# Hybrid GLA and gated-delta layer on one core: length sums in the input stage, delta-rule pairs pipelined by hand, linear attention by units, w_out in halves

## The chip, the core and the metric

The kernel runs on one core of a Trainium2 chip. The time is the device time of one execution in microseconds. The engines are PE (matmuls), PEld (its weight loads), DVE (vector), ACT (activations and copies), POOL (GpSimd) and SP (a queue that issues most DMAs). Each executes its own instructions in order.

## The reference, cut to what matters

One decoder layer for 2048 prompt tokens and 8 samples of 8 tokens (2112 columns). One projection feeds two recurrences: gated linear attention (GLA) and the gated delta rule (GDN). Their outputs are normed, gated and multiplied by `w_out`; a layer norm and a SwiGLU network follow.

```python
h = einsum('btd,de->bte', x, w_in)                    # q,k,v,gates of GLA, conv inputs of GDN, ...
dq = l2_norm(silu(conv(q part))) * DK ** -0.5          # l2_norm: x * rsqrt(sum(x*x) + 1e-6), per head
dk = l2_norm(silu(conv(k part)))
a_mat = eye + strict(beta_i * (k_i . k_j) * exp(gcum_i - gcum_j))
u, w = solve(a_mat, [v * beta, k * beta * exp(gcum)])
delta = u - w @ s
o = (q * exp(gcum)) @ s + (q k^T * gamma) @ delta
s = exp(gcum_last) * s + (k * exp(gcum_last - gcum))^T @ delta
o = rms_norm(o) * silu(gate)
```

## The kernel before, in words

The tokens are cut into 17 units: unit 0 is the 64 sample tokens, units 1 to 16 are 128 prompt tokens each. Eight blocks hold two prompt units each; block 0 also holds unit 0.

The input stage (`phase_in`) goes three times over 704 columns, each in two halves of 352. For each of 12 groups of convolution channels (`f`) and each half, `product` runs 24 matmuls into a PSUM tile `p`. `conv` then copies it to `hb` on ACT, does three multiply-adds into `cv` on DVE, takes Silu on ACT (line 93, `cv<-cv`) and stores it to DRAM. The small columns (decays, beta, gate rank) are a further product of 24 matmuls for each half, into a PSUM tile `g` of which there are two. All other projections follow through `seven` (lines 226 to 228).

The recurrences follow. `phase_gla` and `phase_gdn` are generators that are advanced by turns, one block each. In GDN, `proj` of a block loads q and k, and `unit` makes them of unit length in place, 512 columns at a time:

```python
ptt(sq, x, x, TT.mult)                                        # POOL
nc.tensor.matmul(ps, lhsT=ones, rhs=sq, start=True, stop=True) # PE, line 811
act(rt, ps, AF.Ln, bias=epsl)                                 # ACT
act(rt, rt, AF.Exp, scale=-0.5, bias=lnq[:, g:g + 1])         # ACT
vtt(x, x, rt, TT.mult)                                        # DVE
```

`decays` reads the summed log decays back from DRAM to all partitions (`R`) and takes exponents. `prepare` makes the matrices of a unit (`y`, `yh`, `at`, `kh`, `ke`, `qe`), with k k^T, q k^T and transposes through the one PSUM bank `sc`. `invert` is called for seven levels, for the two units of a block by turns: a matmul group, a copy to `P` on ACT (line 888), two matmul groups, and two predicated copies on DVE (lines 897 and 898). `residual` (its copy `Rs`) and `correct` finish the inverse, and `advance` carries the state through the unit. The tiles `yh`, `yl`, `D` and `DT` have two buffers each, so a block's inversion needs the block ahead of it to be through with them.

The output stage (`phase_out`) loads `w_out` in eight chunks through the two staging buffers `wraw`, scales each on DVE and splits it in a high and a low half (`o0h`, `o0l`, `o1h`, `o1l`), then handles the units in order (`project`). `phase_ffn` is the rest.

The program text sets the order of emission, but a scheduler of the framework reorders the instructions of each engine by its own timing; data and buffers bound it.

Of the kernel before, what the change touches and what calls it, by code (L numbers as in the profile page):

```python
# [20 lines left out]
NS = 64  # L21
# [79 lines left out]
def hybrid_layer(ctx: ExitStack, tc: tile.TileContext, I, O):  # L101
# [41 lines left out]
    if "og" in O:  # L143
# [3 lines left out]
                             for nm, n in (("qk", 4), ("v", 4), ("gt", 8), ("dq", 12)))  # L147
    sm_d = dram.tile([40, NTOK], F32, name="sm")
    grow_d = [dram.tile([4, T], F32, name=f"gr_{b}") for b, (_, T, _) in enumerate(blocks)]
# [9 lines left out]
    c_nb = cols.tile([128, NU, 4], F32, name="c_nb")  # L159
    c_G = cols.tile([64, 4], F32, name="c_G")  # L160
# [5 lines left out]
    def load_quad(pool, tag, src, gain):  # L166

        wh, wl = (pool.tile([128, 8, 512], F32R, name=tag + p, tag=tag + p, bufs=1) for p in "hl")
# [7 lines left out]
        return wh, wl  # L176
# [91 lines left out]
    def phase_in(stack):  # L268
# [52 lines left out]
        def conv(ib, i, f, ps):  # L321
# [23 lines left out]
            nc.scalar.dma_start(out=dq_d[f][:, t0:t0 + FN], in_=cv)  # L345

# [5 lines left out]
        for ib in range(3):  # L352
            if ib:
                ws = load_pair(pw, I["w_p"][0], plain=True)
                xs = load_x(ib)
            for p in range(6):
                if p:
                    ws = load_pair(pw, I["w_p"][p], plain=True)
                for j, c in enumerate("ab"):
                    w = [cols_of(ws[c + d]) for d in "12"]  # L360
                    for i in range(2):
                        ps = psp.tile([128, 512], F32, name="p", tag="p")[:, :FN]
                        product(ps, w, i)
                        conv(ib, i, 2 * p + j, ps)
# [15 lines left out]
            for i in range(2):  # L380
                ps = psg.tile([128, 512], F32, name="g", tag="g")[:64, :FN]
                product(ps, [[(lambda k, d=d, t=t: t[:, 4 * d + k, :]) for t in (wsh, wsl)] for d in range(2)], i)
                sm = p4.tile([64, FN], F32, name="sm", bufs=1)
                nc.scalar.copy(sm, ps)
                t0 = FT * ib + FN * i
                ST.dma_start(out=sm_d[:, t0:t0 + FN], in_=sm[:40])
# [7 lines left out]
        ST.dma_start(out=O["pconv"].rearrange("(f p) c -> p f c", p=128), in_=halo)  # L394


    def phase_gla(stack, more=None, general=False):
# [19 lines left out]
        if not general:  # L417

            gsc = w1.tile([40, 3], F32, name="gsc")
            nc.sync.dma_start(out=gsc[32:40, :], in_=I["gates"])  # L420
            nc.vector.tensor_tensor(gsc[32:40, 1:2], gsc[32:40, 1:2], gsc[32:40, 0:1], op=TT.mult)
            act(gsc[32:40, 2:3], gsc[32:40, 2:3], AF.Exp)
# [18 lines left out]
        if not general:  # L441
            ats = [p1.tile([128, 4, 128], F32, name=f"at{i}", bufs=1) for i in range(2)]
            lows = p1.tile([128, 2, 24], F32, name="lows", bufs=1)

            grs = p1.tile([128, 320], F32, name="grs", bufs=1)
            for t in ats + [lows, grs]:
# [8 lines left out]
        def log_sig(w, rows, T, nm):  # L455

            e = p1.tile([128, 320], F32, name="ls_" + nm, tag="ls", bufs=1)[rows, :T]
            act(e, w, AF.Abs)
            nc.vector.tensor_scalar(w, w, 0.0, None, op0=TT.min)
            act(e, e, AF.Exp, scale=-1.0)  # L460
            act(e, e, AF.Ln, bias=1.0)
            return e

        def proj(b):
# [4 lines left out]
            if not general:  # L469
                wr = p1.tile([40, 320], F32, name="wr", bufs=1)  # L470
                R8 = slice(32, 40)
                nc.sync.dma_start(out=wr[R8, :T], in_=sm_d[32:40, c0:c0 + T])
                nc.vector.tensor_scalar(wr[R8, :T], wr[R8, :T], gsc[R8, 0:1], gsc[R8, 1:2],
                                        op0=TT.mult, op1=TT.add)
                lr = p1.tile([40, 320], F32, name="lr", bufs=1)
                vtt(lr[R8, :T], wr[R8, :T], log_sig(wr[R8, :T], R8, T, "r"), TT.subtract)
                nc.vector.tensor_scalar(lr[R8, :T], lr[R8, :T], gsc[R8, 2:3], None, op0=TT.mult)
                gr = grs
# [828 lines left out]
```

## Time and profile before

| what | us |
|---|---|
| median of three runs (2832.56, 2833.11, 2841.64) | 2833.11 |
| the profiled execution, device time | 2829.82 |
| its span, first to last instruction | 2827.7 |
| PE busy in the span | 2665.6 |
| input stage, to | 633 |
| recurrences, from 633 to | 1113 |
| output stage, from 1113 to | 1384 |
| feed-forward stage, from 1384 to | 2828 |

The stage borders are read from the timeline: the last input product on PE, the first transpose of the output stage, the first product of the feed-forward network. A busy PE holds the modelled length of each matmul, so a PE that is busy in part of a stretch may also be waiting for the clock. PEclk of 1.00 is 2.4 GHz and 0.50 is 1.2 GHz.

### The profile page before, as it was taken

Reading aid. Unit: us, or ns where it says so; the run is one execution under the profiler, and the core shown is the slowest. Engines: PE = TensorE matmul, PEld = TensorE weight load, DVE = VectorE, ACT = ScalarE, POOL = GpSimd, SP = SyncE. Lnnn points to the kernel's source line nnn. Section 1 sums busy time; section 2 is a strip of 40 time slices with the busy share of each in tenths; the row PEclk is TensorE's granted clock in tenths of the full one; section 3 lists DMA queues with packets and bytes.
Section 4 is the critical chain, followed back from the end, with each engine's and each line's share of the span. In section 5 each row is a group of like instructions: output and inputs, shape, how many; then the busy total and the mean of one; then the engine's idle time right before and its main releaser. Section 6 shows DMA issues by size and latency. Waiting matters only on the chain.

```text
span 2827.7 us, 45495 instructions
## 1 busy us (share of the span) xinstructions
PE 2665.6 (94%) x16362; PEld 2435.2 (86%) x16362; DVE 1982.8 (70%) x3160; ACT 1241.3 (44%) x2660; POOL 1176.9 (42%) x1185
## 2 busy tenths in 40 slices
PE   8999999997888887999799999999999999999996
PEld 8999999995767675777799999999999987887885
DVE  7868768655678766686677788777877743555664
ACT  5545445434455553343344453444444432334442
POOL 6534325324344431354555559655665500210111
PEclk9999999996899998999899999999999999999998
DMA  7345344324533223667732346323432243536652
GB/s 258 126 152 186 121 144 157 108 101 126 148 98 99 65 70 102 188 205 240 239 117 101 112 147 203 114 101 124 140 107 103 100 144 131 202 131 244 214 200 85
DMA packets 244232, 406.60 MB, mean 144 GB/s; under 512 B 27900, under 2 KB 202460, under 8 KB 223132
## 3 DMA queue, kind: packets, MB, share of 16 engines
q1 hardware_dynamic: 195900, 364.22, 39.0%
q10 hardware_dynamic: 48096, 39.38, 4.2%
q8 instruction: 131, 2.15, 0.3%
q14 instruction: 105, 0.86, 0.1%
HBM read 305.01 MB, written 98.51 MB: 143 GB/s over the span
## 4 chain that ended last, share of the span: by engine, by line
PE 48%; DMA 2%; DVE 2%; POOL 1%; issue 1%; ACT 0%; SPq 0%; POOLq 0%; ACTq 0%; DVEq 0%
PE p L227 10%; PE p L228 10%; PE p L226 10%; PE p L1203 4%; PE p L1205 4%; PE p L1204 4%; PE g L1203 2%; PE g L1205 2%; PE g L1204 2%; DMA x1T<-x1T 1%; DMA xr<-x1T 1%; POOL xr L131 1%; DVE xl L128 0%; DMA wr<-in_w_dn 0%; DVE wl L128 0%
## 5 line engine op out<-in xcount | busy, mean ns | idle before, releaser
L128 DVE TENSOR_TENSOR wl<-wr,wh 128x512 fp32r<-128x512 f32 x652 | 595.1, 916 | 337.8 <-ACT wh L182 335.4
L226 PE MATMUL p<-xh,wh 128*128 128x352 f32 x2520 | 814.3, 323 | 10.2 <-ACT x1T L1096 5.0
L227 PE MATMUL p<-xl,wh 128*128 128x352 f32 x2520 | 815.1, 323 | 4.1 <-DVE xl L128 4.1
L228 PE MATMUL p<-xh,wl 128*128 128x352 f32 x2520 | 814.4, 323 | 0.3 <-DVE wl L128 0.3
L182 ACT CAST wh<-wr 128x512 fp32r<-128x512 f32 x652 | 401.1, 620 | 582.1 <-PE p L227 274.8
L226 PEld LDWEIGHTS p<-xh,wh 128*128 128x128 f32 x2520 | 474.6, 188 | 11.6 <-ACT x1T L1096 5.4
L227 PEld LDWEIGHTS p<-xl,wh 128*128 128x128 f32 x2520 | 474.8, 188 | 5.9 <-DVE xl L128 5.6
L228 PEld LDWEIGHTS p<-xh,wl 128*128 128x128 f32 x2520 | 474.8, 188 | 0.8 <-DVE wl L128 0.8
L128 DVE TENSOR_TENSOR t<-t,p 128x352 f32<-128x352 f32 x630 | 318.7, 518 | 199.0 <-PE p L228 197.3
L131 POOL TENSOR_TENSOR wt<-wr 128x512 f32<-128x512 f32 x180 | 243.9, 1355 | 242.8 <-DVE wl L128 211.7
L182 ACT CAST wh<-wt 128x512 fp32r<-128x512 f32 x270 | 167.5, 621 | 311.7 <-PE p L227 280.5
L1028 POOL TENSOR_SCALAR mv<-mv 128x1 f32<-128x1 f32 (+1 forms) x34 | 22.8, 674 | 505.6 <-DVE mv L1027 505.6
L128 DVE TENSOR_TENSOR wl<-wt,wh 128x512 fp32r<-128x512 f32 x270 | 202.7, 751 | 19.0 <-ACT wh L182 15.8
L1203 PE MATMUL p<-wh,hh 128*128 128x512 f32 x528 | 208.8, 395 | 0.0
L1204 PE MATMUL p<-wl,hh 128*128 128x512 f32 x528 | 208.7, 395 | 0.0
L131 POOL TENSOR_TENSOR wt<-wr,wt 128x512 f32<-128x512 f32 x90 | 119.4, 1326 | 212.2 <-DVE wl L128 212.0
L1205 PE MATMUL p<-wh,hl 128*128 128x512 f32 x528 | 204.5, 395 | 0.0
L316 PE MATMUL p<-xh,wh 128*128 128x352 f32 x576 | 186.2, 324 | 10.9 <-ACT xh L182 10.9
L317 PE MATMUL p<-xl,wh 128*128 128x352 f32 x576 | 186.3, 323 | 0.0
L318 PE MATMUL p<-xh,wl 128*128 128x352 f32 x576 | 186.2, 323 | 0.0
L131 POOL TENSOR_TENSOR t<-t 128x352 f32<-128x352 f32 x132 | 159.5, 1210 | 59.4 <-ACT t L93 35.3
L332 DVE SCALAR_TENSOR_TENSOR cv<-hb,cw,cv 128x352 f32<-128x352 f32 (+1 forms) x216 | 153.3, 715 | 40.2 <-ACT cv L330 22.6
(280 smaller groups left out, 4816.1 us busy)
## 6 DMA issues: line engine op xcount, KB each, us to landing
wr<-in_w_gu SPq DMA_DIRECT2D x66, 1024.0 KB, 4.9
wr<-in_w_dn SPq DMA_DIRECT2D x55, 1024.0 KB, 4.9
wr<-in_w_p SPq DMA_DIRECT2D x42, 1024.0 KB, 5.1
hid<-t SPq DMA_DIRECT2D x132, 176.0 KB, 1.8
xr<-in_xT SPq DMA_DIRECT2D x96, 176.0 KB, 4.6
dq<-cv ACTq DMA_DIRECT2D x72, 176.0 KB, 2.9
xr<-x1T SPq DMA_DIRECT2D x72, 176.0 KB, 3.6
hr<-hid SPq DMA_DIRECT2D x66, 192.0 KB, 3.4
```

The costliest lines, as they stand in the source:

```text
L128: nc.vector.tensor_tensor(out, a, b, op=op)
L131: nc.gpsimd.tensor_tensor(out, a, b, op=op)
L182: nc.scalar.copy(h[:, :N], raw)
L226: nc.tensor.matmul(ps, lhsT=h[:, ks], rhs=x[k][0], start=k == 0, stop=False)
L227: nc.tensor.matmul(ps, lhsT=h[:, ks], rhs=x[k][1], start=False, stop=False)
L228: nc.tensor.matmul(ps, lhsT=l[:, ks], rhs=x[k][0], start=False, stop=k == 3)
L316: nc.tensor.matmul(ps, lhsT=h(k), rhs=x[k][0], start=n == 0, stop=False)
L317: nc.tensor.matmul(ps, lhsT=h(k), rhs=x[k][1], start=False, stop=False)
L318: nc.tensor.matmul(ps, lhsT=l(k), rhs=x[k][0], start=False, stop=n == 7)
L1203: nc.tensor.matmul(p, lhsT=hh[:, ts], rhs=wd[i][0], start=f == 0, stop=False)
L1204: nc.tensor.matmul(p, lhsT=hh[:, ts], rhs=wd[i][1], start=False, stop=False)
L1205: nc.tensor.matmul(p, lhsT=hl[:, ts], rhs=wd[i][0], start=False, stop=f == NF - 1)
```

## The change

It has four parts.

1. Length sums. `lengths` squares each of the first eight `cv` tiles of a half on ACT and adds the sums of its 128 rows into one row of a PSUM tile `g`, by a matmul with a selector of 8 columns. `store_rows` stores the eight rows to DRAM (`nm`). `rows` takes their logarithm and adds minus half of it to the log decays (in the rows that go to `R`, and in the columns `c_nb`), so that k and q needn't be scaled. What that leaves unscaled in q is put right in the norm of the output stage (`c_r`, `c_rq`). `unit` is gone.
2. GDN pairs. `mix` is replaced by a loop over groups (pairs of units, and the sample unit as the fourth group): between the two `advance` calls of a group four steps of the next group's inversion are emitted, and the group after that is prepared at the end. `yh`, `yl`, `D`, `DT` and `P` have four buffers now. q, k and v are loaded by the unit.
3. GLA advances by units; its sample unit comes after the eighth prompt unit.
4. `w_out` has two pools. The first half is loaded from `phase_gdn`, one chunk after each group; the second in the output stage.

```diff
+        def lengths(f, nps, cv):
+            sq = p4.tile([128, FN], F32, name="sq")
+            nc.scalar.activation(sq, cv, AF.Square)
+            r = (f + 4) % 8
+            nc.tensor.matmul(nps[:8, :FN], lhsT=sel[:, 7 - r:15 - r], rhs=sq, start=f == 0, stop=f == 7)
...
+        def rows(b):
...
+            act(nr[R8, :T], nr[R8, :T], AF.Ln, bias=epsl[R8])
...
+            nc.vector.scalar_tensor_tensor(rr[R4, :T], nr[R4, :T], -0.5, grs[R4, :T], op0=TT.mult, op1=TT.add)
+            for u in us:
+                u0, C = units[u]
+                o = u0 - c0
+                ST.dma_start(out=grow_d[u][:, 0:C], in_=rr[R4, o:o + C])
+                ST.dma_start(out=grow_d[u][:, C:], in_=grs[R4, 7:64:8] if u == 0 else grs[R4, o + C - 1:o + C])
...
+                nc.vector.scalar_tensor_tensor(nb, ct[:C, 64:68], -0.5, ct[:C, 36:40], op0=TT.mult, op1=TT.add)
+                vtt(nb, nb, ct[:C, 0:4], TT.subtract)
...
+                vtt(c_r[:C, u, :], ct[:C, 64:68], ct[:C, 68:72], TT.subtract)
+                act(c_rq[:C, u, :], c_r[:C, u, :], AF.Exp, scale=0.5, bias=lnq[:C])
+                ptt(c_r[:C, u, :], c_rq[:C, u, :], c_rq[:C, u, :], TT.mult)
...
-            def unit(x, N, g):
-                sq = pe.tile([128, 512], F32, name="sq")[:, :N]
-                ptt(sq, x, x, TT.mult)
-                ps = bank("sc")[:, :N]
-                nc.tensor.matmul(ps, lhsT=ones, rhs=sq, start=True, stop=True)
...
+        for n, us in enumerate(groups):
+            if n + 2 < len(groups) and blk[n + 2] > 1:
+                rows(blk[n + 2])
+            steps = inversion(groups[n + 1]) if n + 1 < len(groups) else iter(())
+            for i, u in enumerate(us):
+                for _ in range(4):
+                    next(steps, None)
+                if u == 0:
+                    advance_samples(ws.pop(u))
+                else:
+                    advance(u, ws.pop(u))
+                yield
+            for _ in steps:
+                pass
+            next(more, None)
+            start(n + 2)
...
-            return pa.tile([128, FN], F32, name="xr", bufs=8)
+            return pa.tile([128, FN], F32, name="xr", bufs=7)
```

What that does to the engines' orders shows at three places. First PE at the start of the program, before the change; `p` is a convolution product, `g` the small columns.

```order
L316 MATMUL p<-xh,wh 128x352
L316 MATMUL g<-xh,wsh 64x352
L317 MATMUL p<-xl,wh 128x352
L318 MATMUL p<-xh,wl 128x352
L316 MATMUL p<-xh,wh 128x352
L317 MATMUL g<-xl,wsh 64x352
L317 MATMUL p<-xl,wh 128x352
L318 MATMUL p<-xh,wl 128x352
```

Of the change, the place on PE where the first row of length sums stands, after 43 matmuls of products; `sel` is the selector.

```order
L319 MATMUL p<-xl,wh 128x352
L320 MATMUL p<-xh,wl 128x352
L360 MATMUL g<-sq,sel 8x352
L319 MATMUL p<-xl,wh 128x352
L320 MATMUL p<-xh,wl 128x352
L318 MATMUL p<-xh,wh 128x352 x2
```

The length sums hold both `g` tiles until the eighth channel group is done, so the 24 matmuls of the small columns that stood among the first 60 stand behind the 16th sum now. Each of the 48 sums stands among later products: in the second and third pass 43 to 62 product matmuls behind the last one of its own product.

Next PE in the recurrences of the change: the end of the eighth GLA unit (`g<-v,kz` is its state update), with GDN's state products (`seq`, `po`) and k k^T of the samples (`sc<-k`) around it.

```order
L920 MATMUL seq<-S,ke 128x128 x4
L836 MATMUL sc<-k 64x64 x2
L644 MATMUL g<-v,kz 128x128 x4
L936 MATMUL po<-S,qe 128x128
L528 MATMUL g<-ident,vf 64x128
L890 LDWEIGHTS P_7796
L890 MATMUL inv<-D,P_7796 128x64
```

The recurrences take some 3700 rows of PE's order. The next GLA prompt unit (its gate product `g<-gar,wup`) stands some 1800 rows further on; between them GLA has its sample unit only, and GDN goes on alone. The other eight GLA units stand behind that, the last two behind GDN's last state update. Before, GLA's 16 units stood among the first five GDN blocks, and the last three had none beside them.

Last SP in the recurrences: of the change, the third chunk of `w_out` (`Sh` and `state_gdn` are the samples' state, which uses the same two staging buffers).

```order
L525 DMA vf<-v 128x4x128
L486 DMA gar_8631<-sm 16x256
L174 DMA wraw<-in_w_out 128x2x512
L947 DMA Sh<-in_state_gdn 128x8x128
L754 DMA wr<-sm 8x256
L772 DMA gr_111<-grs 4x8x1
```

Two chunks stand in the input stage, this one near the start of the recurrences, the fourth in their middle, and four (the second half) behind that. Before, the first two of the eight chunks stood among the loads of the last GDN block, and the rest in the output stage:

```order
L798 DMA vf<-dq 128x4x128 x2
L790 DMA cv<-dq 128x4x256
L172 DMA wraw<-in_w_out 128x2x512 x2
L1047 DMA lng<-in_ln 128x1024
L1048 DMA lnb<-in_ln 128x1024
L172 DMA wraw<-in_w_out 128x2x512
```

## Rows read from the trace of the kernel before

**Rows 1.** The page: span, and engines' busy time.

```profile
span 2827.7 us, 45495 instructions
PE 2665.6 (94%) x16362; PEld 2435.2 (86%) x16362; DVE 1982.8 (70%) x3160; ACT 1241.3 (44%) x2660; POOL 1176.9 (42%) x1185
```

**Rows 2.** Busy time of each engine by stage; PEclk is the granted clock.

```profile
core 0: us, PE busy (x) PEld busy (x) DVE busy (x) ACT busy (x) POOL busy (x), PEclk, DMA share, GB/s
0.00:50.00 50.00, 38.83 (x225) 37.28 (x226) 35.09 (x65) 29.84 (x70) 27.07 (x41) 1.00 0.81 286
50.00:633.00 583.00, 583.00 (x3647) 580.04 (x3646) 438.38 (x691) 283.21 (x584) 237.96 (x291) 1.00 0.42 139
633.00:1113.00 480.00, 392.26 (x3618) 331.04 (x3616) 339.11 (x733) 237.20 (x587) 183.57 (x263) 0.88 0.34 97
1113.00:1384.00 271.00, 237.29 (x1100) 185.32 (x1100) 189.87 (x265) 108.85 (x366) 122.54 (x138) 0.93 0.71 218
```

**Rows 3.** The same, stretches of the recurrences.

```profile
633.00:735.00 102.00, 82.80 (x535) 63.23 (x533) 53.52 (x120) 38.45 (x98) 38.92 (x74) 0.72 0.45 126
...
773.00:941.00 168.00, 138.31 (x1332) 119.47 (x1331) 136.64 (x295) 100.89 (x258) 71.84 (x104) 0.95 0.33 94
...
1002.00:1113.00 111.00, 88.27 (x1002) 76.83 (x1000) 72.92 (x162) 48.96 (x112) 29.84 (x35) 0.95 0.23 69
```

**Rows 4.** Timeline of PE in the recurrences: start, length, instruction.

```profile
1014.14 1.02 PE L811 MATMUL sc<-sq,ones 128*128 128x512 f32 x2
1015.00 0.39 PE L937 MATMUL po<-S,qe 128*128 128x128 f32 x2
```

**Rows 5.** Timeline of PE in the input stage.

```profile
233.84 0.32 PE L316 MATMUL p<-xh,wh 128*128 128x352 f32 x1
234.00 0.32 PE L317 MATMUL p<-xl,wh 128*128 128x352 f32 x1
```

**Rows 6.** Timeline of ACT in the input stage, second pass, first and third product.

```profile
227.37 0.45 ACT L327 COPY hb<-p 128x352 f32<-128x352 f32 x1
...
232.56 0.50 ACT L93 ACTIVATE cv<-cv 128x352 f32<-128x352 f32 x1 [0.84 <-DVE cv L332]
...
244.58 0.50 ACT L93 ACTIVATE cv<-cv 128x352 f32<-128x352 f32 x1 [2.18 <-DVE cv L332]
```

**Rows 7.** PE's groups and waits between 8 and 30 us.

```profile
L316 PE MATMUL p<-xh,wh 128*128 128x352 f32 x26 | 8.8, 353 | 10.9 <-ACT xh L182 10.9
...
L316 PE MATMUL g<-xh,wsh 128*64 128x352 f32 x8 | 3.2, 396 | 0.2 <-ACT wsh L306 0.2
```

**Rows 8.** Groups of DVE, POOL and ACT in the recurrences: busy, mean ns | idle before.

```profile
L128 DVE TENSOR_TENSOR cv<-cv,rt 128x512 f32<-128x512 f32 x32 | 25.6, 799 | 13.3 <-ACT rt L93 10.5 <-issue 1.8 <-POOL ckh L131 0.7
...
L473 DVE TENSOR_SCALAR wr<-wr,gsc 8x256 f32<-8x256 f32 x7 | 4.1, 587 | 1.4 <-DMA wr<-sm 1.3
...
L128 DVE TENSOR_TENSOR ckh<-sc,c_nb 64x4 f32<-64x4 f32 x1 | 0.1, 144 | 0.0
...
L131 POOL TENSOR_TENSOR sq<-cv 128x512 f32<-128x512 f32 x32 | 34.5, 1081 | 39.9 <-PE sc L811 23.1 <-PE sc L801 14.4 <-PE inv L884 2.3
...
L131 POOL TENSOR_TENSOR ckh<-R,c_nb 128x4 f32<-128x4 f32 x16 | 3.4, 218 | 21.9 <-DVE kh L128 19.5 <-DMA R<-gr 2.2
...
L93 ACT ACTIVATE rt<-rt,lnq 128x512 f32<-128x512 f32 x32 | 23.3, 728 | 0.4
```

**Rows 9.** Timeline of PE, start of the output stage; in brackets the wait.

```profile
1113.00 0.69 PE L1073 MATMUL pt<-ident,on 64*128 64x64 f32 x4 [4.33 <-DVE on L128]
...
1135.79 0.69 PE L249 MATMUL pw<-o1h,oh 128*64 128x512 f32 x1 [3.87 <-ACT o1h L174]
...
1141.65 0.45 PE L249 MATMUL pw<-o0h,oh 128*128 128x512 f32 x1
```

**Rows 10.** DMA issues in the recurrences (KB each, us to landing), then the chain that ended last.

```profile
R<-gr SPq DMA_DIRECT2D x16, 256.0 KB, 3.2
...
1689.10 3.29 DMA xr<-x1T
```

More of the change, by code (lines that the diff above doesn't have):

```diff
@@ L380, in phase_in @@
             for i in range(2):
[L381 to L386, printed above, removed]
+                ps = psg.tile([128, 512], F32, name="g", tag="g")
+                product(ps[:64, :FN], [[(lambda k, d=d, t=t: t[:, 4 * d + k, :]) for t in (wsh, wsl)] for d in range(2)], i)
+                store_rows(ps, 64, sm_d, ib, i)
             for n, (to, c) in enumerate(dst):
@@ L706, in phase_gla @@
         for b in range(NBLK):
-            mix(b, proj(b))
-            yield
+            r = proj(b)
+            if b == 0:
+                r0 = r
+            yield from mix([u for u in blocks[b][2] if u], r)
+            if b == 3:
+                yield from mix([0], r0)
         S = state["S"]
@@ L828, in prepare @@
[L828 removed]
+            return gbt[:C, :, :C], eR[:, :, :C], ckh, eGl
+        def prepare(u):
             u0, C = units[u]
             smp = u == 0
[L832 to L834 removed]
+            w = {}
+            q, k, vf = (new(n)[:, :, :C] for n in ("q", "k", "vf"))
+            for t, n in ((q, 0), (k, 4), (vf, 8)):
+                nc.sync.dma_start(out=t, in_=dq_d[n:n + 4, :, u0:u0 + C].rearrange("h p t -> p h t"))
+            w["q"], w["k"] = q, k
+            gb, eR, ckh, w["eGl"] = decays(u)
+            w["eR"] = eR
+            pt = pmt("sc")
+            for h in range(4):
+                nc.tensor.transpose(pt[:C, h, :], vf[:, h, :], ident)
+            w["v"] = new("vt")
+            nc.scalar.copy(w["v"][:C], pt[:C])
@@ L1015, in phase_gdn, with inversion @@
-        for b in range(NBLK):
-            mix(b, proj(b))
-            yield
+        ws = {}
+        def inversion(us):
+            C = units[us[0]][1]
+            for lv in range(3 if C == NS else 7):
+                for u in us:
+                    invert(lv, C, ws[u])
+                yield
+            for u in us:
+                residual(C, ws[u])
+            yield
+            for u in us:
+                correct(C, ws[u], "D", "t1", F16)
+            for u in us:
+                correct(C, ws[u], "t1", "Dr", F32)
+            yield
@@ new lines, in phase_gdn, with start @@
+        groups = [[u, u + 1] for u in range(1, NU, 2)]
+        groups.insert(3, [0])
+        blk = [us[0] // 2 for us in groups]
+        def start(n):
+            if n < len(groups):
+                for u in groups[n]:
+                    ws[u] = prepare(u)
+        rows(0)
+        start(0)
+        rows(1)
+        for _ in inversion(groups[0]):
+            pass
+        start(1)
+        for n, us in enumerate(groups):
[5 more added lines that the diff above has]
+                    next(steps, None)
+                if u == 0:
+                    advance_samples(ws.pop(u))
+                else:
+                    advance(u, ws.pop(u))
+                yield
+            for _ in steps:
+                pass
+            next(more, None)
+            start(n + 2)
@@ L1018, in phase_gdn @@
+        for _ in more:
+            pass
         ST.dma_start(out=O["pgdn"].rearrange("h d v -> d h v"), in_=state["S"])
-        yield
     def layer_norm(pool, v, C, g, b, spare=False):
@@ L1238, in hybrid_layer @@
                 pass
-        with ExitStack() as stack:
-            finish(stack)
+        out = ExitStack()
+        wo, more = load_out(out, gain, 0)
+        for _ in more:
+            pass
+        finish(rest, out, wo)
 GT, X1T = 3, 1
```

311 lines of the change are left out of this document (131 added, 180 removed).

## The prediction

> **What bounds the kernel now.** I read the page first [rows 1]: PE is busy for 2665.6 of 2827.7 us, so the question is where it isn't, and whether its busy time is real work. The windows by stage answer that [rows 2]. From 50 to 633 us PE is busy for all of 583 us at a granted clock of 1.00: the input stage is bound by PE, and whatever is added to PE there is paid in full. In the first 50 us PE waits for data (38.8 busy). The recurrences take 480 us, and no engine is full: PE 392 at a mean clock of 0.88, DVE 339 (0.706 of the stretch), ACT 237, POOL 184. That stage is bound by chains that cross engines, and by how well two recurrences fill each other's gaps. Its stretches differ [rows 3]: from 633 to 735, where the samples' chain runs almost alone, DVE is busy for 0.52; from 773 to 941, where GLA and GDN run side by side, 136.64 of 168, or 0.813; from 1002 to the end, where GLA is through and GDN goes alone, 72.92 of 111, or 0.657. The output stage is nearly full of PE work (237 of 271) but for its start and end.
>
> **The change, part by part.** *Length sums added to the input stage.* PE gets 48 matmuls of f32 with 352 columns (8 channel groups, 3 passes, 2 halves). The nearest row is the old sum of squares, f32 with 512 columns in two passes: started at 1014.14, the next instruction at 1015.00 [rows 4], so 0.86 us, or 0.59 for 352 columns; 48 x 0.59 = 28.3 us. A product matmul of 352 columns starts each 0.16 us [rows 5], but it is one pass over operands split in high and low. No row has f32 with eight columns of weights, so the far ends are 48 x 0.16 = 7.7 and 48 x 0.86 = 41; I take 28.3, since passes and columns are the same kind as in rows 4. PE has no gap there to hide it.
>
> *Do these sums wait?* A sum stands 43 to 62 product matmuls behind its own product, so 6.9 to 9.9 us, and up to 1.2 more for sums between. What it needs: the first product of the second pass is read at 227.37, and its Silu ends at 233.06, after 5.7 us. The third product ends 48 x 0.16 = 7.7 us later, at 235.05, and its Silu ends at 245.08, after 10.0 us [rows 6]. The Square adds about 0.5, as long as a Silu. So 6.2 to 10.5 are needed where 6.9 to 11 are given: 3 us of waits in all, between 0 and 8. ACT gets 48 x 0.5 = 24 us in a stage where it is busy for 283 of 583, which hides it; without that cover it would come out as just these waits.
>
> *Small columns later.* While PE waits at the start (10.9 us, for x), 24 matmuls of small columns fill its time (eight in each of three lines) [rows 7]. Their tiles are held by the sums now, so they come in a full stretch: 24 x 0.16 = 3.8 us, less if products move up in their place. Between 0 and 3.8; I take 3. Input stage: 28.3 + 3 + 3 = +34, between +29 and +42 at the price taken.
>
> *Taken out of the recurrences.* POOL loses 32 squares (34.5 us) and two half as wide, ACT 64 activations of some 0.7 us, PE 32 x 0.86 = 27.5 us, DVE 32 multiplies (25.6 us) and two half as wide, 26.4 in all [rows 8]. Added on DVE: one operation of 8 rows for each block at 0.59, so 5 us, and three of four columns for each of 17 units at 0.144, so 7 us. DVE's work goes from 339 to 339 - 26 + 5 + 7 = 325 us. POOL and ACT, at half of the stretch or less, are not what fills it.
>
> *Order of the recurrences.* PE loses 27.5 us of work but wasn't full, so I price the stage by how full DVE gets. By the order, 44 in 100 of DVE's instructions of this stage stand where GLA pauses. The rest, 0.56 x 325 = 182 us, has GLA beside GDN and takes the fill of rows 3, 0.813: 224 us. The paused part, 143 us of work, would at the old fill of GDN alone, 0.657, take 218. Four buffers let a pair's inversion start while the pair ahead is corrected and advanced, and the samples' chain now lies among pairs. I take a fill halfway, 0.735: 195 us. Together 419 in place of 480, so -61. Bounds: 0.813 throughout gives 400 (-80), 0.657 in the pause 442 (-38). What is late next is the end: the last two GLA units stand behind GDN's last state update, with nothing beside them.
>
> *Loads of `w_out`.* In the output stage the first transpose starts at 1113.00, the second unit's products at 1141.65: 28.6 us for a unit where steady ones take some 16 (the stage's 271 us over 17). In it PE waits for the second half's chunks, 3.87 us at most at once [rows 9]. The first half is there in advance now, and two chunks of the second wait in staging. At least that wait goes (-4), at most 28.6 - 16 and the gap of 4.33 ahead (-17); I take -11.
>
> *At no cost.* SP issues 91 DMAs more, and each unit's `R` comes by two stores and a load that lands in 3.2 us [rows 10]; rows are made two groups ahead, which hides it. Without that cover it is about 6 us for each of 8 pairs, and is part of the first rival. The norm of the output stage gets two POOL operations for each unit, 0.22 each [rows 8]; loads run ahead there, and PE is the bound. Uncovered: 17 x 0.44 = 7 us. The feed-forward stage has seven raw buffers instead of eight: its second block now waits 3.29 us for such a load [rows 10], at most as much again at each of two entries.
>
> *Sum.* The profiled execution took 2829.8 us, 2.1 more than its span and 3.3 less than the median of the runs: 2829.8 + 34 - 61 - 11 = 2792, as a median 2795.
>
> *A rule against it.* PE's granted clock is 0.72 from 633 to 735, where its work is sparse, and 0.95 from 773 on [rows 3]; the levels are 1.2 and 2.4 GHz, so it spent more than half of that first stretch at the lower one. The Trainium skill, "TensorE: Matmul & The Clock Gate", Part 1 (the HAM clock gate), says that the throttled rate is the default and that activity releases it. This trace agrees, with 0.72 and 0.95. By that rule the pause of GLA, with less on PE, could go at the lower level for long, and the time would be that of the third rival.
>
> **The rivals.** *First: the hand order brings nothing.* A scheduler already reorders all of it, and the old order too started the next inversion behind the last correction; the pause of GLA makes half of the stage like its old end. Then fill stays at 0.706: 325 / 0.706 = 460, -20. 2829.8 + 34 - 20 - 11 + 3.3 = 2836, no change. Against it: the samples' 102 us at a fill of 0.52 go in among pairs.
>
> *Second, on the other side: the sums stall PE.* PE is in order, so a sum whose Square is late stops all products behind it. If each of 48 comes 1.5 us late, 72 us in place of 3: 2864. For it: needs of up to 10.5 us against places of 6.9 upward [rows 6]. Against it: a stall gives DVE and ACT time to catch up. It decides from 50 us of waits, 1 us for each sum.
>
> *Third: the clock falls in the pause.* If the paused 195 us go at 0.72 in place of 0.95, they take 257: +62, 2857. It decides at a clock of 0.77 there. For it: PE has neither GLA nor the old sums then. Against it: GDN alone, from 1002 on, has 0.95.
>
> *Fourth: more than forecast.* With inversions of two pairs in flight DVE is full to 0.90 throughout: 361 us, -119, so 2737.
>
> **How the numbers follow.** Forecast 0.62, first rival 0.13, second 0.08, third 0.07, fourth 0.10. The forecast's own range takes the terms' bounds: 2829.8 + 29 - 80 - 17 + 3 = 2765 to 2829.8 + 42 - 38 - 4 + 3 = 2833. About 0.3% (8.5 us) is what a measurement can tell from no change. Faster: 0.62 less the 0.02 of its upper end, and 0.10, so 0.70. Same: 0.13 + 0.02, and a small second rival 0.01, so 0.16. Slower: 0.14. The range for 8 in 10 leaves out most of the second and third rivals: 2742 to 2842.
>
> **What would show it.** The input stage should end at 662 to 675, with PE full; 48 sums at 0.59 each, and few waits for the Square. The recurrences should take 400 to 442 us, with GLA absent from the middle, DVE at 0.7 or more there and at 0.8 at both ends, and no sum on POOL. The first output unit should take under 20 us, and the feed-forward stage its 1444 us. I am wrong if sums wait for ACT by over 1 us each, if the middle's clock is under 0.8, or if the stage's DVE fill stays at 0.7.

## The result: slower by 2.6%, and the profile after

The changed kernel takes 2912.11 us (median of 2908.22 to 2917.14), the kernel before 2835.01 on the same chip: a ratio of 1.0262 with a 95% interval of 1.0246 to 1.0278. Forecast were 2795, with 0.14 for slower. Its profiled execution has a span of 2909.4 us; these are its page's first lines, which answer to [rows 1].

```profile
span 2909.4 us, 45610 instructions
PE 2687.0 (92%) x16390; PEld 2447.1 (84%) x16390; DVE 1964.3 (68%) x3185; ACT 1235.3 (42%) x2671; POOL 1134.2 (39%) x1197
```

DVE lost 18 us of work, PE gained 21, and the span grew by 82: most of that is neither. The windows by stage, as in [rows 2] (busy time of each engine with its instructions, PEclk, DMA share, GB/s), show where.

```profile
0.00:50.00 50.00, 31.78 (x166) 29.21 (x167) 33.54 (x57) 26.87 (x63) 22.03 (x40) 0.93 0.80 276
50.00:692.00 642.00, 635.74 (x3819) 594.34 (x3818) 442.76 (x702) 312.48 (x648) 225.60 (x295) 1.00 0.38 127
692.00:1162.00 470.00, 368.77 (x3533) 327.41 (x3531) 326.36 (x763) 209.83 (x547) 153.29 (x237) 0.84 0.39 106
1162.00:1472.00 310.00, 250.91 (x1089) 197.30 (x1090) 175.40 (x252) 98.75 (x353) 123.62 (x167) 0.88 0.58 174
1472.00:2373.00 901.00, 888.13 (x5545) 885.40 (x5544) 700.70 (x990) 398.95 (x727) 541.20 (x410) 0.99 0.37 127
2373.00:2909.00 536.00, 511.67 (x2246) 413.42 (x2244) 285.56 (x423) 188.41 (x336) 68.45 (x52) 0.98 0.49 173
```

To compare kernels, the stages are cut at the same events on PE in each: the last product of the input stage, the first transpose of the output stage (a wait ahead of it counts with the recurrences), the first gate product, the first down product. Us, from the timelines:

| kernel | input | recurrences | output | gate and up | down | median, ratio to before (95%) |
|---|---|---|---|---|---|---|
| before | 635.9 | 477.2 | 261.7 | 904.5 | 548.5 | 2835.01 |
| after | 691.9 | 470.1 | 309.7 | 901.4 | 536.3 | 2912.11, 1.0262 |
| difference | +56.0 | -7.0 | +48.0 | -3.1 | -12.2 | forecast: +34, -61, -11, 0, 0 |

Where PE waits in the whole of the changed kernel (sum, times, longest):

```profile
PE pw L251 <- ACT oh L1109: 50.9, 16, 10.2
PE p L318 <- ACT xh L184: 17.6, 2, 8.9
PE pt L1104 <- DVE on L128: 15.4, 2, 12.6
...
PE g L360 <- ACT sq L358: 6.5, 11, 1.4
```

The second is the wait for x at the start, 10.9 before [rows 7]; the third is the output stage's start, the last the length sums. The first, 16 times in the 17 units of the output stage, is new: one of them lasts 10.2 us, the others 2.7 on average (before, there were two such waits, 4.4 us in all). The timeline of PE there shows it; a period is from one `px` row to the next, 17.37 us.

```profile
1241.81 1.03 PE L1125 MATMUL px<-ident,xt 128*128 128x128 f32 x8
1245.71 1.03 PE L1104 MATMUL pt<-ident,on 128*128 128x128 f32 x8
1249.42 0.80 PE L251 MATMUL pw<-o0h,oh 128*128 128x512 f32 x1 [2.68 <-ACT oh L1109]
...
1259.18 1.03 PE L1125 MATMUL px<-ident,xt 128*128 128x128 f32 x8
...
1263.08 1.03 PE L1104 MATMUL pt<-ident,on 128*128 128x128 f32 x8
```

Before, the same rows of two units, with other rows of PE left out; the period is 12.95 us:

```profile
1164.41 1.03 PE L1094 MATMUL px<-ident,xt 128*128 128x128 f32 x8
1166.68 0.60 PE L1073 MATMUL pt<-ident,on 128*128 128x128 f32 x4
1169.92 0.60 PE L1073 MATMUL pt<-ident,on 128*128 128x128 f32 x4
1177.36 1.03 PE L1094 MATMUL px<-ident,xt 128*128 128x128 f32 x8
```

There the transposes come in two groups of four, each among the products of the unit ahead, and wait for nothing. After the change, all eight transposes `pt` of a unit stand right before that unit's own products `pw`, so the gating on DVE and the split to `oh` on ACT lie open between them. That was to be read from the order of the changed kernel before it ran, and the prediction took no notice of it.

And the length sum, in the input stage. It has two records (x2) and lies between the products of 302.12 and 303.06, which stand 0.94 apart in place of 0.16: 0.78 for a sum, not 0.59. All 37 sums that didn't wait cost the same.

```profile
302.12 0.32 PE L319 MATMUL p<-xl,wh 128*128 128x352 f32 x1
302.37 0.76 PE L360 MATMUL g<-sq,sel 128*8 128x352 f32 x2
303.06 0.43 PE L320 MATMUL p<-xh,wl 128*128 128x352 f32 x1
```

### The profile page after: what moved, and what is told of

It reads as the page before. It is cut to its first block, busy times and chain, and to the rows that moved or that the text cites. A ratio compares the mean times of both kernels' runs of the same rounds, so it can differ in the third digit from the quotient of the medians.

```text
span 2909.4 us, 45610 instructions
## 1 busy us (share of the span) xinstructions
PE 2687.0 (92%) x16390; PEld 2447.1 (84%) x16390; DVE 1964.3 (68%) x3185; ACT 1235.3 (42%) x2671; POOL 1134.2 (39%) x1197
## 5 line engine op out<-in xcount | busy, mean ns | idle before, releaser
L228 PEld LDWEIGHTS p<-xh,wh 128*128 128x128 f32 x2520 | 474.3, 188 | 10.2 <-ACT xh L184 5.3
```

Source lines behind the costliest of these rows:

```text
L228: nc.tensor.matmul(ps, lhsT=h[:, ks], rhs=x[k][0], start=k == 0, stop=False)
```

## The experiments

The table has all eighteen, the columns as above.

| run | input | recurrences | output | gate and up | down | median | ratio (95%) |
|---|---|---|---|---|---|---|---|
| a_on3 | 692.6 | 471.7 | 249.0 | 902.6 | 536.1 | 2851.96 | 1.0058 (1.0040 to 1.0076) |
| a_pipe | 692.2 | 472.0 | 255.7 | 902.6 | 534.4 | 2858.05 | 1.0081 (1.0052 to 1.0110) |
| a_sides | 691.6 | 462.4 | 309.6 | 900.4 | 546.6 | 2912.91 | 1.0285 (1.0244 to 1.0326) |
| b_sides | 639.1 | 503.6 | 258.3 | 915.0 | 534.0 | 2849.96 | 1.0049 (1.0032 to 1.0066) |
| a_sumr | 667.4 | 476.7 | 306.4 | 900.1 | 536.4 | 2891.56 | 1.0217 (1.0191 to 1.0243) |
| a_noord | 691.9 | 473.2 | 307.6 | 900.9 | 535.5 | 2907.55 | 1.0267 (1.0241 to 1.0293) |
| a_noord2 | 693.2 | 482.2 | 306.7 | 900.8 | 534.6 | 2923.88 | 1.0339 (1.0300 to 1.0378) |
| a_glaend | 693.9 | 477.8 | 311.9 | 902.2 | 535.5 | 2919.55 | 1.0310 (1.0284 to 1.0336) |
| a_unit | 638.2 | 478.6 | 304.0 | 900.9 | 537.9 | 2860.76 | 1.0088 (1.0066 to 1.0111) |
| a_early | 692.1 | 459.8 | 249.8 | 902.6 | 536.4 | 2839.49 | 1.0022 (1.0002 to 1.0042) |
| a_best | 658.4 | 470.0 | 251.9 | 902.6 | 535.9 | 2819.08 | 0.9932 (0.9913 to 0.9950) |
| a_best2 | 657.7 | 465.6 | 249.8 | 903.2 | 538.0 | 2812.16 | 0.9912 (0.9893 to 0.9930) |
| a_unit2 | 638.5 | 467.8 | 255.2 | 902.0 | 535.2 | 2804.96 | 0.9908 (0.9889 to 0.9926) |
| a_nogla | 692.8 | 407.3 | 309.9 | 899.8 | 537.0 | 2849.51 | 1.0046 (1.0018 to 1.0074) |
| a_inv3 | 693.7 | 465.9 | 304.0 | 901.6 | 536.9 | 2902.82 | 1.0247 (1.0217 to 1.0276) |
| a_sc2 | 693.6 | 460.9 | 307.4 | 902.5 | 535.2 | 2901.27 | 1.0241 (1.0212 to 1.0271) |
| a_warm | 692.0 | 465.3 | 308.5 | 901.6 | 539.6 | 2912.22 | 1.0281 (1.0262 to 1.0299) |
| a_final | 637.4 | 464.9 | 255.8 | 901.5 | 535.9 | 2798.71 | 0.9872 (0.9851 to 0.9893) |

### The output stage: one buffer, or the order written out

```diff
-                on = pi.tile([128, 512], F32, name="on", bufs=2)
+                on = pi.tile([128, 512], F32, name="on", bufs=3)
```

> The changed kernel with one more buffer for the loaded outputs (on, three in place of two), nothing else. In the order of PE each unit's transposes then stand among the products of the unit ahead, in place of right before their own products. Theory: the output stage's loss is that place: the chain transposes, gating on DVE, split on ACT is exposed once a unit (3.2 us by 17 units) and the clock falls with it. Then the stage goes from 338 to about 275 us and the whole from 2912 to about 2850. Rival: the two POOL operations added to each norm and the chunks of w_out set the stage, then it stays above 325 us and the whole above 2900.

The stage went from 309.7 to 249.0 us and the whole to 2851.96, as the theory of order has it. PE's timeline in a_on3, to be held against the two above: the two groups of four `pt` lie among other rows of PE (left out here) and wait for nothing, and the period is 12.95 us.

```profile
1258.36 1.04 PE L1125 MATMUL px<-ident,xt 128*128 128x128 f32 x8
...
1260.64 0.60 PE L1104 MATMUL pt<-ident,on 128*128 128x128 f32 x4
...
1263.87 0.60 PE L1104 MATMUL pt<-ident,on 128*128 128x128 f32 x4
...
1271.31 0.93 PE L1125 MATMUL px<-ident,xt 128*128 128x128 f32 x7
```

Its waits, and its window. The wait for `oh` fell from 50.9 to 1.6 us, and the granted clock rose from 0.88 to 0.96. In the two windows PE's idle time fell from 59.1 us to 18.8 (some other waits grew), and its busy time, for as many matmuls, from 250.9 to 230.2: of the 61 us, 40 are waits and 21 are the clock.

```profile
PE pw L251 <- ACT oh L1109: 1.6, 2, 0.9
```

```profile
1164.00:1413.00 249.00, 230.20 (x1088) 182.17 (x1088) 173.83 (x252) 99.00 (x353) 120.13 (x166) 0.96 0.70 215
```

With the order mended the stage is 12.7 us shorter than before. What the loads of `w_out` bring is seen in its first unit, from the first transpose to the second unit's products: 28.65 us before [rows 9], 18.60 in a_on3, and 26.3 in b_sides (below), which loads `w_out` as before.

```profile
1164.24 0.69 PE L1104 MATMUL pt<-ident,on 64*128 64x64 f32 x4 [12.77 <-DVE on L128]
...
1182.84 0.50 PE L251 MATMUL pw<-o0h,oh 128*128 128x512 f32 x1
```

The Trainium skill, "Perfetto Trace Analysis", Optimization Strategy, says that a gap which repeats on the engine that should be full can mean too few buffers for the next tile; these traces agree, with 16 waits that one buffer took away.

```diff
+        ready = norm(0)
         for u in range(NU):
-            project(u)
+            now, ready = ready, norm(u + 1) if u + 1 < NU else None
+            project(u, *now)
```

> The changed kernel with the norm of the next unit written ahead of the products of the unit at hand, and four buffers in place of three for the split outputs (oh, ol). By the theory of order it gives what the extra buffer gives: an output stage of about 275 us, 2850 in all; perhaps some us less, since both halves of the next unit are ready early (2840). By the rival (POOL's operations and the chunks) above 2900.

The stage takes 255.7 us: the same cure by other means.

Which part of the change put the transposes together isn't settled, but the other runs, each of which undid one part or two, rule out much of it. In a_sides, a_noord, a_noord2, a_glaend and a_unit the stage stays at 304 to 312 us and the transposes of every unit, or of all but the first, stand together. So it is not the pools' sides, the hand order, the four buffers, the place of GLA's sample unit, or the length sums. a_unit has no POOL operations added to the norm either, and PE's wait is still there:

```profile
PE pw L251 <- ACT oh L1101: 45.9, 17, 5.1
```

What no run undid is, above all, `w_out` in two pools, GLA by units, loads by the unit, and the seven raw buffers.

### The input stage: what a sum costs

```diff
-            sq = p4.tile([128, FN], F32, name="sq")
+            sq = p4.tile([128, FN], F32R, name="sq")
```

(and the selector likewise)

> The changed kernel with the squares and the selector of the length sums in the format of the split products (f32r) in place of plain f32: squares are rounded a little, PE makes one pass over 352 columns and needn't change format between the products and the sum. Theory: a sum costs 0.78 us of PE because of the passes of plain f32 and some 0.1 us at each change of format; now it costs 0.16 to 0.2. Then the input stage ends 28 to 30 us earlier, at about 663 in place of 692, and the whole takes 2883. Rival: the sums' place in the order and the wait for the Square set the loss; then the stage ends above 685 and the whole takes 2905 or more.

The stage ended 24.5 us earlier. A sum now takes one place in the row of products, 0.16 us:

```profile
286.51 0.32 PE L319 MATMUL p<-xl,wh 128*128 128x352 f32 x1
286.67 0.32 PE L362 MATMUL g<-sq,sel 128*8 128x352 f32 x1
286.83 0.32 PE L320 MATMUL p<-xh,wl 128*128 128x352 f32 x1
```

48 x (0.78 - 0.16) = 29.8, less 5.5 because the sums now wait 12.0 us for the Square in place of 6.5: 24.3. So most of the price is that of the format: the sums' waits are 6.5 us against 29.8.

The small columns were written ahead of the convolution products:

```diff
+            for i in range(2):
+                ps = psg.tile([128, 512], F32, name="g", tag="g")
+                product(ps[:64, :FN], ...)
+                store_rows(ps, 64, sm_d, ib, i)
             nps = []
```

> The changed kernel with three buffers for the loaded outputs (2852 us) and the small columns of each pass written ahead of the convolution products, so that they have the PSUM tiles before the length sums do. In the order of PE they then stand among the first sixty matmuls again. Theory: the input stage loses 9 to 10 us at its start because PE has nothing to fill the wait for x; now it gets them back: input stage to 683, the whole 2843. Rival: the start is set by when x and the chunks of w_out land, and nothing changes: 2852.

The total fell by 12.5 us against a_on3, but not for the expected reason: the input stage still ends at 692.1. Its start did get faster, with 76 matmuls on PE in the first 30 us where a_on3 has 46 (30 x 0.16 = some 5 us), but a sum of the second pass then waits 3.9 us for its Square. The recurrences, whose code is the same, are 12 us shorter (459.8 against 471.7). So 12 us is how far this stage moves when its own code is left alone; no smaller difference in it is read as an effect below.

Then the first part of the change was undone alone.

```diff
-                        if f < 8:
-                            lengths(f, nps[i], cv)
...
+            for g, t in enumerate((q, k)):
+                sq = pe.tile([128, 4, 128], F32, name="sq")[:, :, :C]
+                ptt(sq, t, t, TT.mult)
+                ps = pmt("sc")[:, :, :C]
+                nc.tensor.matmul(ps, lhsT=ones, rhs=sq, start=True, stop=True)
...
```

> The changed kernel with its first part undone alone: no length sums in the input stage, k and q brought to unit length in the recurrences by the old square, sum, logarithm, exponent and multiply, now for each unit's q and k; no length terms in the decays and in the output norm. Theory: the sums cost the input stage 56 us (48 by 0.78, 6.5 of waits, the rest at the start, where the small columns come too late to fill it), and the recurrences get only the work back at a fill that doesn't change, about 20 us. Then the input stage ends at about 637, the recurrences take 490 and the whole 2876. Rival: the work that left the recurrences is worth there what the forecast said, so that they go to 520 us or more, and the whole stays at 2905 or above.

The input stage gave back 53.7 us, and the recurrences took 8.5 more, though PE, DVE, ACT and POOL all had the old work again, DVE 14 us of it. The 8.5 are within the scatter of 12, so what that work is worth there is small, but not measured. The first part costs 51 us of the whole by the two medians.

### The recurrences: order, buffers, work, banks, clock

> The changed kernel with the hand order of the delta-rule pairs undone in the text: each group is prepared, inverted and advanced before the next is begun, as before the change; the four buffers of yh, yl, D, DT and P stay. Theory of the scheduler (the first rival of the prediction): it reorders by readiness anyway, so the recurrences keep their 470 us, within 10. Theory of the forecast: the hand order fills gaps; without it the recurrences take 490 us or more.

```diff
+            start(n)
+            for _ in inversion(us):
+                pass
             for u in us:
...
```

473.2 us against 470.1: the hand order brings nothing that shows.

```diff
-              "yh": 4, "yl": 4, "D": 4, "DT": 4,
+              "yh": 2, "yl": 2, "D": 2, "DT": 2,
```

> The same as the run without hand order, and the buffers of yh, yl, D, DT and P back at two, so that a pair's inversion can't begin until the pair ahead is through with them. If buffers are what the gain of the recurrences hangs on, they take 490 us or more; if what was saved is the work of the length sums alone, 470 within 10.

482.2, between the two bounds; 9 us beyond the run with four buffers is within the stage's scatter.

```diff
-            if b == 3:
+            if b == NBLK - 1:
                 yield from mix([0], r0)
```

> The changed kernel with GLA's sample unit behind its sixteenth prompt unit in place of behind the eighth, so that GLA's prompt units needn't wait in the middle for the staging buffers that GDN's samples and the chunks of w_out hold. Theory: the pause of GLA is where the forecast gain was lost; then the recurrences get 20 to 40 us shorter (430 to 450 of 470). Rival: GLA then ends early and GDN goes alone at the end as it did before the change; the recurrences keep 470 us within 10. A second rival: GLA's sample unit stands alone behind everything and costs its 10 to 20 us: 480 to 490.

477.8: GLA's prompt units now run on to 1043 us without the pause, and the stage isn't shorter. The pause of GLA isn't where the gain went.

```diff
+                if u > 2 and not general:
+                    nc.scalar.dma_start(out=on_d[0][u], in_=v[:C])
+                    continue
```

> The changed kernel with fourteen of GLA's sixteen prompt units cut to loading, transposing and storing v (their decay projections stay; scans, exponents, products and state are left out), so that GDN has the engines nearly to itself. This takes 14 x 4.6 = 64 us of work from DVE and some 60 from PE. Theory: GDN's own chain sets the recurrences, and work that lies beside it is worth little: 440 us or more of 470. Rival (the prediction's way to count): DVE's work at an unchanged fill of 0.69 sets them, 64 / 0.69 = 92 us less: 378 or less.

407.3, between the two, so neither number held. DVE has 58 us less work, the stage is 63 us shorter, 6.6 of them the wait ahead of the output stage (12.61 to 6.05 us). With GLA nearly gone DVE is filled to 268.00 of 407, or 0.66, and GDN still takes 87% of the time. So GDN, without most of GLA's work beside it, still needs some 400 us while no engine is full: a chain of dependent steps is the likely reason, which this run suggests and doesn't prove. A microsecond of DVE's work taken out was worth about one, not 1 / 0.69, and PE, ACT and POOL lost work with it.

```profile
693.00:1100.00 407.00, 321.75 (x3111) 282.04 (x3110) 268.00 (x640) 182.31 (x464) 125.84 (x195) 0.81 0.45 124
```

Some of this chain is seen in who waits for whom in the changed kernel's recurrences: ahead of 50 of the 98 copies to `P` ACT waits for PE, and ahead of 31 of the 98 predicated copies to `DT` DVE waits for PE (sum, times, longest). These waits come to 79 of 470 us, so they don't make up the chain by themselves.

```profile
ACT P L887 <- PE inv L883: 47.6, 50, 2.3
```

```profile
DVE DT L896 <- PE inv L893: 31.3, 31, 5.2
```

```diff
-PBK = {"sc": 1, "inv": 2, "seq": 2, "po": 1}
-POT = "po"
+PBK = {"sc": 1, "inv": 3, "seq": 2}
+POT = "seq"
```

> The changed kernel with three PSUM banks for the inversions in place of two; the bank of GDN's outputs (po) is given up for it, and they go through the two state banks (seq). Theory: GDN's chain is held by the banks that the inversions share (a matmul group waits until the group two ahead has been read), and the recurrences take 450 or less. Rival: the chain is the latency from PE to ACT to PE to DVE in each level, which banks don't change: 470 within 10, or more where po now waits.

And with two for `sc`, two for `inv`, two for `seq`:

> The same with the bank given to the preparation (sc, two in place of one), through which each unit's transposes, k k^T and q k^T go one after the other. Theory: preparation is late for the inversions because of the one bank, and the recurrences take 450 or less. Rival: 470 within 10.

465.9 and 460.9 us, 4 and 9 less and within the scatter: banks are not shown to hold it, though both point the same way.

```diff
+            for t in (q, k):
+                ps = pmt("sc")[:, :, :C]
+                nc.tensor.matmul(ps, lhsT=ones, rhs=t, start=True, stop=True)
```

> The changed kernel with 34 idle matmuls put into the recurrences: the old sum over 128 rows, 512 columns of f32, on each unit's q and k, whose result nobody reads. It adds some 27 us to PE's work and nothing elsewhere. Theory: with the old sums gone PE's granted clock fell in the middle of the recurrences (0.85 from 800 to 1000 us, against 0.91 in the run that has the sums back there), and part of the gain was lost to slower matmuls in the chain; then the clock rises to about 0.9 there, and the recurrences take no more than 470 us in spite of the added work. Rival: the clock in the middle doesn't follow this work, it stays at 0.85, and the recurrences take 475 us or more.

First the window of the changed kernel's pause, then the same one of a_warm.

```profile
800.00:1000.00 200.00, 165.59 (x1660) 147.85 (x1659) 129.13 (x303) 78.04 (x205) 68.79 (x101) 0.84 0.38 104
```

```profile
800.00:1000.00 200.00, 174.95 (x1754) 147.46 (x1753) 133.81 (x313) 78.84 (x207) 70.53 (x107) 0.91 0.40 106
```

The granted clock rose from 0.84 to 0.91, and the stage took 465.3 us with 34 idle matmuls more; the whole took 2912.22 where the changed kernel took 2912.11. That is no gain that can be read; but the stage has room for such matmuls, within its scatter, so that taking 27.5 us of sums off PE could bring little there. How much of this is the clock and how much is that PE waits for the chain anyway, no run tells. The Trainium skill, "TensorE: Matmul & The Clock Gate", Part 1, says that activity releases the lower rate; these two rows agree.

### The down projection: where its tiles lie

> The changed kernel with the SBUF sides of the output and feed-forward pools put back as they were before (pa left; pi, p3, po, pw, p4 right); the output stage keeps its bad order. Theory: the feed-forward stage is 21 us shorter after the change because its weights and activations lie elsewhere in SBUF, and each product of 512 columns starts 0.2275 us after the last in place of 0.2335. Then this run takes about 2932 us and a feed-forward stage of 1444 us. Rival: the gain is from the seven raw buffers and the order that they give; then it stays at 2912 and 1423.

> The kernel before with only the SBUF sides of the output and feed-forward pools exchanged (pa right; pi, po, p3, pw, p4 left), eight raw buffers kept. Theory of the sides: the feed-forward stage goes from 1444 to about 1423 us and the whole from 2835 to about 2815, with the pitch of 512-column products at 0.2275 us. Rival (seven raw buffers): no change, 2835. The output stage's order differs a little, plus or minus 8 us.

The edit in both is the `side` of the pools, as

```diff
-        pa = stack.enter_context(tc.tile_pool(reuse_waits=RW, name="pa", bufs=2))
+        pa = stack.enter_context(tc.tile_pool(reuse_waits=RW, name="pa", bufs=2, side="right"))
```

and the reverse. As totals both expectations failed, since the pools also move the recurrences and the gate stage (recurrences of 503.6 us in b_sides, which wasn't followed up, and 462.4 in a_sides, which has lost the 12.6 us wait ahead of the output stage). But the down projection goes with the sides: 548.5 and 546.6 us with `pw` and `p4` right (before, a_sides), 536.3 and 534.0 left (after, b_sides). In 50 us without a wait, at a granted clock of 1.00, PE starts 216 products of 512 columns or 222. First before, a_sides, after and b_sides:

```profile
2309.00:2359.00 50.00, 50.00 (x216) 37.40 (x215) 16.06 (x28) 14.51 (x27) 0.00 (x0) 1.00 0.37 126
```

```profile
2394.00:2444.00 50.00, 50.00 (x216) 37.44 (x215) 16.05 (x28) 14.47 (x27) 0.00 (x0) 1.00 0.37 126
```

```profile
2403.00:2453.00 50.00, 50.00 (x222) 38.35 (x221) 16.46 (x27) 14.50 (x27) 0.00 (x0) 1.00 0.38 132
```

```profile
2346.00:2396.00 50.00, 50.00 (x222) 38.35 (x221) 16.46 (x27) 14.50 (x27) 0.00 (x0) 1.00 0.39 133
```

`pa` went to the other side each time that `pw` and `p4` did, and all addresses moved with it, so which of these counts isn't shown. `pi` and `p3` don't: a_best2, a_unit2 and a_final move those two alone, and their down projection stays at 535 to 538 us.

### Kernels that beat both

> The three edits together: three buffers for the loaded outputs, length sums in the format of the split products, small columns ahead. If each keeps its own gain (60, 24 and 9 us) the whole takes 2912 - 93 = 2819, faster than the kernel before by 0.5%. Rival: the waits of the sums for the Square take the gain at the start back, and it ends at 2828 to 2836, no change from before.

> The same three edits, and the pools of the output stage's inputs on the other SBUF side (pi, p3 right, the feed-forward pool pa opened ahead of them), pw and p4 staying left. Theory: the 12.6 us that PE waits for the first transpose of the output stage are a wait for SBUF that the recurrences hold, and the run with the sides put back had no such wait: 8 us less than without this edit, 2811. Rival: the inputs then sit where GDN's last tiles are and the start gets no shorter: 2819.

> The changed kernel with its first part undone (lengths in the recurrences again, 2861 us), three buffers for the loaded outputs, and the output stage's input pools on the other side. If the gains of the runs apart add up: 2861 - 60 - 6 = 2795, and what is left of the change (order, GLA by units, w_out in halves, pools) with the output stage mended is 1.3 to 1.5% faster than the kernel before. Rival: the output stage or the recurrences give some back, and it takes 2812 or more, as the best run so far.

> The best run so far (lengths back in the recurrences, three buffers for the loaded outputs, pools of the output stage's inputs on the other side: 2805 us) with the second bank for the preparation in place of a bank of its own for GDN's outputs. If the 9 us of recurrences that this bank brought without the lengths hold here too: 2796. With the lengths' sums in the same bank it may bring more, 2790. Rival: outputs then wait in the state banks, no change: 2805.

As totals the gains added up: 2819.08 where 2819 were expected, 2812.16 for 2811, 2804.96 for 2795 (10 us less gained, an output stage of 255.2 for 249 among them), 2798.71 for 2796. Two of these sums were met in part by luck: the 9 us of the small columns had not shown in the input stage of a_early but do in a_best (658.4 for a_sumr's 667.4), and the wait that a_best2 was to take away only fell from 13.9 us to 8.2. The last step, 6 us, has recurrences 3 us shorter, within their scatter. a_final joins a_unit, a_on3, the pools of a_best2 and the bank of a_sc2; it keeps the hand order, GLA by units, and `w_out` in halves, and is 1.3% faster than the kernel before. By stages it is 32 us shorter: 12.6 in the down projection, so by the pools' sides; 12.3 in the recurrences, which is as much as they scatter; 5.9 in the output stage; 3.0 in gate and up; and 1.5 longer in the input stage. Its edits against the changed kernel are those shown, with `pa` opened ahead of the output stage's pools, and for these

```diff
-        pi, p3 = (stack.enter_context(tc.tile_pool(reuse_waits=RW, name=n, bufs=2)) for n in ("pi", "p3"))
+        pi, p3 = (stack.enter_context(tc.tile_pool(reuse_waits=RW, name=n, bufs=2, side="right")) for n in ("pi", "p3"))
```

## Why the prediction was wrong

By span the change added 82 us where 38 were to go, an error of 120: output stage 59, recurrences 54, input 22, feed-forward -15.

*At no cost* is the step that failed most. It let the output stage pass because "loads run ahead there, and PE is the bound". PE was the bound before only because each unit's transposes stood among the products of the unit ahead. In the changed order all eight stand behind them, right before their own products, and 16 waits, 50.9 us in all, with a lower granted clock cost 61 us; a third buffer takes both away. The two POOL operations, which the step did price, play no part in it: a_unit has the loss without them. The term for `w_out`, -11, was right in itself: the first unit went from 28.65 us to 18.60 with the order mended. What in the change tipped the scheduler's order is not settled; that a third buffer tips it back is shown.

*Order of the recurrences* failed next. DVE's work was right, 326 us where 325 were forecast. The fill was not: 0.735 for the pause and 0.813 beside GLA. GLA's eighth unit ends at 848 us in the changed kernel and its ninth begins near 1037; up to the pause, in it and behind it DVE was busy for 118.79 of 156 us, 123.56 of 189 and 84.01 of 125.

```profile
692.00:848.00 156.00, 112.76 (x987) 100.08 (x986) 118.79 (x266) 84.17 (x219) 67.01 (x110) 0.80 0.45 119
...
848.00:1037.00 189.00, 159.54 (x1634) 140.04 (x1633) 123.56 (x301) 71.66 (x190) 60.95 (x93) 0.85 0.39 106
1037.00:1162.00 125.00, 96.46 (x917) 87.29 (x915) 84.01 (x197) 54.00 (x139) 25.32 (x34) 0.87 0.30 88
```

That is 0.65 in the pause, as GDN alone had it before (0.657), and 0.72 beside GLA. At the forecast's fills the same work takes 168 and 249 us, not 189 and 281: the stretches beside GLA cost 32 us, more than the pause with 21. Over the stage the fill is 0.69, the prediction's own sign of being wrong, and the first rival, which left it at 0.706, gave 460 for a stage of 470. But that rival's way to count was wrong too: fill isn't what sets the stage. It was 0.71 with the work put back (340 of 478.6) and 0.66 with GLA taken out; it seems to follow from the work and from GDN's own need of about 400 us, whose cause stays open. The four buffers and the hand order, from which the gain was to come, brought 9 and 3 us, no more than scatter. The third rival, the clock in the pause, was there in half: 0.84 from 800 to 1000 us, where 0.95 was taken and 0.77 was to decide. The end grew worse too. GLA's last two units do stand behind GDN's last state update, as "what is late next" said. But the wait for the first transpose, 12.61 us where it was 4.33 [rows 9], isn't theirs: a_sides has them there as well and no wait, so it goes with the side of the pools, which the prediction left out. First the changed kernel, then a_sides:

```profile
1161.98 0.69 PE L1104 MATMUL pt<-ident,on 64*128 64x64 f32 x4 [12.61 <-DVE on L128]
```

```profile
1153.72 0.27 PE L706 MATMUL g<-ident,low 128*1 128x128 f32 x1 [1.78 <-ACT on L262]
1154.00 0.62 PE L1104 MATMUL pt<-ident,on 64*128 64x64 f32 x4
```

*Length sums*: right in mechanism, too small in size. 48 x 0.78 = 37.4 for 28.3; waits 6.5 for 3; the start 9.4 (166 matmuls in 50 us for 225, by 0.16) for 3. That makes 53 of 56. The price was taken from sums that stood among f32 matmuls, while here each has split products on both sides: a_sumr shows that the format is what costs; that the scaling missed the change of format between neighbours is likely, not shown. Of the start only some 3.5 us are the small columns, as forecast: in the first 30 us PE has 100 matmuls before, 47 after, and 69 in a_unit, which has no sums, so 22 x 0.16 go with the sums. What else slows the start is open. The second rival's mechanism, sums that stall PE, did not come: 6.5 us where 50 were to decide.

*Feed-forward at its 1444 us*: 15 less. Of these 12 are the sides of the pools, which the change moved and the prediction didn't price. The gain is luck.

Open are the cause of the scheduler's choice, what holds GDN at about 400 us and what fewer steps would gain, how the place of a pool changes the start-to-start time of products, and the 2.7 us left of the input stage.

## What to carry to other kernels

Before a stage is costed at nothing, read in the new order whether the instructions that feed the bound engine still stand a whole unit ahead of their use; if not, price the chain between them once for each unit. A stage in which no engine is full is not priced by work over fill: find out what it takes with the suspected filler removed, and value work beside the chain at its own length or less. Work moved out of such a stage into one where an engine is full is paid there in whole: here 54 us, for 8.5 that the stage's scatter doesn't let be told from nothing.

## What was not expected of the hardware

A matmul of f32 with 352 columns and 8 columns of weights cost 0.78 us among split products, where 0.59 was worked out from f32 neighbours; in the split format it cost 0.16. Products of 512 columns started 216 or 222 times in 50 us at the same granted clock of 1.00, by the SBUF sides of the feed-forward pools. And 34 matmuls without a purpose, put into the recurrences, raised the granted clock from 0.84 to 0.91 in their middle and made the stage no longer.
